# A side-input projection, a variance and a set of stores are moved in a two-layer encoder kernel

## The chip, the core and the metric

The kernel runs on one core of one Trainium2 chip. The metric is the device time of one execution in microseconds (us), and what is reported is the median of several runs. Engines are named as in the profile: PE is TensorE (PEld its weight loads), DVE is VectorE, ACT is ScalarE, POOL is GpSimd, SP is SyncE, which here does nothing but issue DMA transfers. A "q" behind an engine's name (SPq) means its instruction queue: an instruction there issues a transfer and the engine itself stays idle.

## The reference

All is float32; the sequence has 1024 positions, the model 1024 features, and there are two layers. Cut to what matters here, a layer `i` computes

```python
x = layer_norm(ALPHA * x + mix(x), ln_mix_g[i], ln_mix_b[i])        # windowed attention, or HGRN2
x = layer_norm(ALPHA * x + swiglu(x, ffn_w_in[i], ffn_w_out[i]), ln_ffn_g[i], ln_ffn_b[i])
x = x + sigmoid(x @ ple_w_gate[i]) * (p[i] @ ple_w_proj[i])

def layer_norm(x, g, b):
    mu = x.mean(-1); var = square(x - mu).mean(-1)
    return (x - mu) * rsqrt(var + eps) * g + b

def swiglu(x, w_in, w_out):
    g, u = split(x @ w_in, 2)
    return (silu(g) * u) @ w_out
```

The hidden width of the feed-forward part is 2816. The side input `p[i]` has 256 features per position, so `p[i] @ ple_w_proj[i]` needs nothing that the layer computes.

## The kernel before

**Layout.** Activations stand transposed: a tile is 128 features by 512 positions, so a tensor is 8 feature tiles (`m` or `k`, 0 to 7) in two halves `h` of the sequence. For precision every float32 operand of a matmul is split into a rounded part `hi` (an ACT copy to fp32r, line 73) and the rest `lo` (a subtraction on DVE or POOL, line 74); `mm3` (line 317) then makes three matmuls of 512 columns, hi by hi, hi by lo, lo by hi.

**A layer's second part, `ffn_ple` (line 663).** The feed-forward products are made by a seven-product scheme on 2 by 2 blocks (products 1 to 7). The stages are, in order:

- `early` (line 688): products 1 and 2 of the first `NA` = 4 hidden tiles `f`, 24 matmuls each. They need only the first half's normed x and are woven (line 891) with `pend`, the mix norm of the second half.
- `layer_norm` with `which` = 0 and `h` = 1 (line 393; "the mixed norm"): the mean on PE (`mu`), a subtraction on DVE and a square on ACT for each of 8 tiles (lines 400 to 405), the squares added up in `v` by DVE and POOL in turn (line 406), `average(var, ones, v)` (line 411), which splits `v` and makes two matmuls, then square root, reciprocal and scaling. Behind each pair of scaled tiles `combine` (line 367) builds the sums and differences `xc` that products 4 to 7 need, splits them, and stores the four y tiles in DRAM from SP's queue (line 390).
- `matmuls_in` (line 768): for each of 22 tiles `f`, products 6, 5, 7 (`mid`), 4, 3 (`tail`) and from `f` = 4 on 1 and 2 (`head`), 84 matmuls per `f`. Behind each pair of tiles `spill` (line 748) forms four differences on POOL, and `w_sums` (line 757) forms sums of output weights; both lie in a list that `store` (line 763) writes to DRAM from SP's queue. The spill of the last pair and its stores come at the very end (lines 782 to 785).
- `matmuls_out` (line 787): 16 loads bring y back (line 794); then for the seven products `p` in `ORDER` and 11 pairs `k`, 12 matmuls each. `take_w` gives out a weight tile `wo` and a hidden tile `hs`, both loaded from DRAM and split; `wo` lies in the pool `hl` of 5 buffers, `hs` in the pool `x` of 16.
- `ple` (line 853), for each half: it loads and splits the side input (`praw`, `p`), and for each of 8 tiles `m` makes 6 matmuls of the side projection `pr` and 24 of the gate `pgps`, then sigmoid, product and sum. `ple(0)` is woven with the second half's output norm (line 897).

**What sets the order.** Weights come by a plan (`ffn_plan`, `plan_all`): a list of steps with a `begin` that starts a load and a function that splits. `take_w` (line 125) hands out the next step and works ahead by `ahead` steps; a step that has a `begin` may start loading up to three steps before it is split (`fetch_w`, line 115). The `pp` and `pg` weights (lines 286 and 287) have no `begin`. `weave(main, side, ratio)` (line 337) lets one generator take `ratio` steps for each step of the other; the tile framework then orders each engine's instructions by its own estimate, the order written here being its priority, and puts in the waits. Each engine and each queue works strictly in that order. In the trace the mean's matmuls of the first layer stand behind 30 matmuls of `early` although they are written behind 12.

## Time and profile before

| | |
|---|---|
| median of 3 runs | 2908.45 us (2905.96 to 2911.57) |
| profiled execution, its own time | 2906.97 us |
| its span in the trace | 2905.2 us |
| mean granted TensorE clock | 0.972 of full speed |
| instructions | 37125 |
| busy share: PE, DVE, POOL, ACT | 93%, 70%, 48%, 44% |
| HBM read, written | 267.18 MB, 76.02 MB |

A profile is one execution. "Busy" is the time in which an engine's instructions ran; matmuls overlap their neighbours, so each of them is recorded longer than the distance to the next. Where an engine stood idle the trace names what released it (`<-`). The clock column of a stretch (PEclk) is the granted share of full TensorE speed.

### The profile page before, as it was taken

The page shows a single profiled execution, that of the slowest core. Times are in us where ns is not written, and L with a number is a line of the kernel's source. Part 1 is how long each engine was busy: PE and PEld are TensorE (multiplying, and loading weights), DVE is VectorE, ACT ScalarE, POOL GpSimd, SP SyncE. Part 2 cuts the span into 40 slices and gives each one's busy share as a digit, 9 for nine tenths or more (in the row PEclk, how much of TensorE's full clock was granted, in tenths as well). Part 3 has the DMA queues.
Part 4 walks back from the last instruction along what each step waited for, and adds up shares of the span by engine and source line. Part 5 has one row for each costly group of instructions (what it writes and reads, how often), then busy time and mean ns, then how long its engine had stood idle before and what let it go on. Part 6 is the DMA issues. An engine that isn't in the chain of part 4 may idle for free.

```text
span 2905.2 us, 37125 instructions
## 1 busy us (share of the span) xinstructions
PE 2707.3 (93%) x12792; PEld 2175.3 (75%) x12792; DVE 2031.5 (70%) x2949; ACT 1278.9 (44%) x2324; POOL 1384.0 (48%) x968
## 2 busy tenths in 40 slices
PE   8999996999998999999998989989879999989999
PEld 6666774788886877787887878878658888868777
DVE  6778878655554757758888888997885555556674
ACT  4555765233333445544344444444533333434452
POOL 4243245666655446653343433421566655553652
PEclk9999997999999999999999999999979999999999
DMA  4111232544447822221121211112344444496133
GB/s 160 48 44 44 71 129 71 182 152 163 145 160 263 302 73 95 98 85 63 57 64 51 66 55 59 66 48 81 107 141 167 152 152 163 170 342 202 41 108 118
DMA packets 191997, 345.66 MB, mean 119 GB/s; under 512 B 21824, under 2 KB 26688, under 8 KB 191808
## 3 DMA queue, kind: packets, MB, share of 16 engines
q1 hardware_dynamic: 191808, 343.29, 34.7%
q8 instruction: 100, 1.64, 0.2%
q14 instruction: 89, 0.73, 0.1%
HBM read 267.18 MB, written 76.02 MB: 118 GB/s over the span
## 4 chain that ended last, share of the span: by engine, by line
PE 67%; DVE 17%; ACT 5%; issue 4%; POOL 4%; DMA 2%; SPq 0%; ACTq 0%; POOLq 0%; DVEq 0%
PE x L318 5%; PE x L320 5%; PE x L319 5%; PE zy L318 3%; PE zy L320 3%; PE zy L319 2%; PE ox L319 2%; PE ox L320 2%; PE ox L318 2%; PE zps L320 2%; PE zps L319 2%; PE zps L318 2%; PE lv L1019 2%; PE s L525 2%; PE oz L320 1%
## 5 line engine op out<-in xcount | busy, mean ns | idle before, releaser
L74 POOL TENSOR_TENSOR w_hz<-r_hz,w_hz 128x512 fp32r<-128x512 f32 x128 | 180.8, 1420 | 329.3 <-ACT w_hz L73 322.7
L74 POOL TENSOR_TENSOR wo<-wraw,wo 128x512 fp32r<-128x512 f32 x132 | 183.7, 1401 | 230.5 <-ACT wo L73 183.5
L74 DVE TENSOR_TENSOR wp<-wraw,wp 128x512 fp32r<-128x512 f32 x204 | 201.2, 986 | 108.9 <-ACT wp L73 107.9
L74 DVE TENSOR_TENSOR hs<-wraw,hs 128x512 fp32r<-128x512 f32 x154 | 185.0, 1226 | 123.8 <-ACT hs L73 123.6
L318 PE MATMUL x<-xc,wp 128*128 128x512 f32 x528 | 213.4, 405 | 46.4 <-ACT xc L73 41.6
L73 ACT CAST wp<-wraw 128x512 fp32r<-128x512 f32 x204 | 127.0, 622 | 245.0 <-PE zy L320 153.9
L319 PE MATMUL x<-xc,wp 128*128 128x512 f32 x528 | 211.9, 401 | 1.5 <-DVE xc L74 1.5
L318 PE MATMUL zps<-xh_n,w_hz 128*128 128x512 f32 x512 | 212.2, 414 | 0.0
L320 PE MATMUL x<-xc,wp 128*128 128x512 f32 x528 | 211.1, 400 | 0.0
L320 PE MATMUL zps<-xh_n,w_hz 128*128 128x512 f32 x512 | 202.3, 395 | 0.0
L319 PE MATMUL zps<-xl_n,w_hz 128*128 128x512 f32 x512 | 201.0, 393 | 0.0
L73 ACT CAST wo<-wraw 128x512 fp32r<-128x512 f32 x154 | 95.1, 620 | 222.2 <-POOL wo L74 78.7
L318 PE MATMUL ox<-hs,wo 128*128 128x512 f32 x352 | 141.4, 402 | 23.4 <-ACT hs L73 23.4
L318 PEld LDWEIGHTS x<-xc,wp 128*128 128x128 f32 x528 | 100.4, 190 | 79.4 <-ACT xc L73 46.7
L319 PE MATMUL ox<-hs,wo 128*128 128x512 f32 x352 | 141.2, 401 | 1.0 <-DVE hs L74 1.0
L320 PE MATMUL ox<-hs,wo 128*128 128x512 f32 x352 | 140.6, 399 | 0.0
L74 DVE TENSOR_TENSOR wp<-s,wp 128x512 fp32r<-128x512 f32 x88 | 91.8, 1045 | 65.1 <-ACT wp L73 65.0
L1019 PEld LDWEIGHTS lv<-Q,ks 128*128 128x128 f32 x768 | 97.8, 191 | 37.0 <-issue 24.3
L1011 ACT COPY ks<-K 128x512 f32<-128x512 f32 x96 | 60.5, 630 | 145.5 <-DVE K L1016 111.1
L1019 PE MATMUL lv<-Q,ks 128*128 128x128 f32 x768 | 105.4, 279 | 20.3 <-DVE tot L1030 10.3
L319 PEld LDWEIGHTS x<-xc,wp 128*128 128x128 f32 x528 | 100.3, 190 | 27.9 <-DVE xc L74 5.2
L320 PEld LDWEIGHTS x<-xc,wp 128*128 128x128 f32 x528 | 100.4, 190 | 24.4
(373 smaller groups left out, 8444.1 us busy)
## 6 DMA issues: line engine op xcount, KB each, us to landing
wraw<-in_wfi_dram SPq DMA_DIRECT2D x192, 256.0 KB, 5.2
wraw<-in_wfo_dram SPq DMA_DIRECT2D x154, 256.0 KB, 4.7
wraw<-h SPq DMA_DIRECT2D x154, 256.0 KB, 5.3
r_hz<-in_whg_dram SPq DMA_DIRECT2D x128, 256.0 KB, 2.6
wraw<-w SPq DMA_DIRECT2D x88, 256.0 KB, 5.3
w<-wraw SPq DMA_DIRECT2D x66, 256.0 KB, 2.0
h<-th SPq DMA_DIRECT2D x66, 256.0 KB, 2.8
r_pg<-in_wpg_dram SPq DMA_DIRECT2D x64, 256.0 KB, 2.8
```

Of the source, the lines that this page charges most:

```text
L73: act.copy(hi, src)
L74: (eng or dve).tensor_tensor(lo, src, f32(hi), op=ALU.subtract)
L318: pe.matmul(ps, lhsT=w[0], rhs=x[0], start=start, stop=False, skip_group_check=free)
L319: pe.matmul(ps, lhsT=w[0], rhs=x[1], start=False, stop=False, skip_group_check=free)
L320: pe.matmul(ps, lhsT=w[1], rhs=x[0], start=False, stop=stop, skip_group_check=free)
L525: pe.matmul(sp[r][:, :n * P], lhsT=qq[rs], rhs=kk[rs], start=i == 0, stop=i == 2)
L1011: act.copy(view(ks, 0, [[2 * B, g], [B, 2], [1, B]]), kv)
L1019: pe.matmul(lv[:, c], lhsT=ks[:, c * P:(c + 1) * P], rhs=view(Qq, c * P, dims), start=True, stop=True)
```

## The change

- The `pp` weights become plan steps with a `begin`, behind product 2 of `f` = 1. A new generator `shares` loads and splits the side input of both halves, makes the 96 projection matmuls of the layer (each weight tile taken once for both halves), copies each result out of PSUM on ACT and stores it to a DRAM tile `pr`. It runs between `early(1)` and `early(2)`; the weave's ratio goes from 2 to 1.
- `ple` loads `pr` back from DRAM and makes only the 24 gate matmuls per `m`. The `pg` weights get a `begin`: one load per `m` into the pool `x`.
- In the mixed norm each square goes into a plain float32 matmul by the matrix `onef` of 1/1024, summed in PSUM; the additions into `v` and the `average` of it are gone there.
- Stores of y, of the hidden tiles and of the weight sums are issued from ACT's queue instead of SP's, those of the last pair in two parts: two tiles at once, the other five behind the first steps of `matmuls_out`.
- In `matmuls_out` the look-ahead goes from 3 to 6 steps, `wo` moves to the pool `x`, and its split is always POOL's.

```diff
@@ ffn_plan @@
                 one(("w", f, 2), w_src(f, 1))
+                if f == 1:
+                    for m in range(KT):
+                        box = []
+                        def begin(m=m, box=box):
+                            raw = wp.tile([P, 4 * P], F32, tag="raw", bufs=3, name="r_pp")
+                            sync.dma_start(raw[:, :2 * P], wpp[li][m])
+                            box.append(raw)
+                        def fin(box=box):
+                            hl = wp.tile([P, 2, HALF], F32R, tag="hl", bufs=5, name="w_pp")
+                            split(hl[:, 0, :2 * P], hl[:, 1, :2 * P], box[0][:, :2 * P])
...
+                        step(("pp", m), begin, fin)
...
-                        w = blocks(pair_of(box[0], "wo", pool if p not in (7,) else None))
-                        hl = fx["pool"].tile([P, 2, HALF], F32R, tag="x", bufs=16, name="hs")
-                        split(hl[:, 0], hl[:, 1], box[1])
-                        return w, (hl[:, 0], hl[:, 1])
+                        for raw, eng, name in ((box[0], pool, "wo"), (box[1], dve, "hs")):
+                            hl = fx["pool"].tile([P, 2, HALF], F32R, tag="x", bufs=16, name=name)
+                            split(hl[:, 0], hl[:, 1], raw, eng)
...
@@ plan_all @@
-                        will(("pp", m), load_tile, wpp[li], m, 2, "pp")
-                        will(("pg", m), load_tile, wpg[li], m, KT, "pg")
...
+                            raw = fx["pool"].tile([P, 2, HALF], F32, tag="x", bufs=16, name="r_pg")
+                            sync.dma_start(raw.rearrange("p c n -> p (c n)"), wpg[li][m])
...
+                        will2(("pg", m), begin, fin)
@@ combine @@
-                    sync.dma_start(fx["y"][m, h], Y[m][h])
+                    act.dma_start(fx["y"][m, h], Y[m][h])
@@ layer_norm @@
+            mixed = which == 0 and h == 1
+            v = None if mixed else T("to", "v")
+            var = (bank or MM)("var") if mixed else None
...
+                if mixed:
+                    sq = T("t0", "sq")
+                    act.activation(sq, ys[m], AF.Square)
+                    pe.matmul(var, lhsT=onef, rhs=sq, start=m == 0, stop=m == KT - 1)
...
-            var = (bank or MM)("var")
-            average(var, ones, v)
+            if not mixed:
+                var = (bank or MM)("var")
+                average(var, ones, v)
@@ spill, store @@
+                    ts = list(zip(ORDER, (a, c, t2, t3, t4, b, d)))
+                    lag.append([(fx["kept"][p, k], t) for p, t in (ts[2:] if rest else ts)])
...
-                            sync.dma_start(dst, src)
+                            act.dma_start(dst, src)
@@ matmuls_in, at its end @@
+                    store()
+                    act.dma_start(fx["kept"][1, FP - 1], sts[FT - 2]["h"][0])
                     yield from tail(FT - 1, sts[FT - 1])
-                    store()
-                    spill(FP - 1, sts[FT - 2], sts[FT - 1])
-                    store()
+                    act.dma_start(fx["kept"][2, FP - 1], sts[FT - 1]["h"][0])
+                    late.append(lambda: spill(FP - 1, sts[FT - 2], sts[FT - 1], True))
@@ matmuls_out @@
-                            w, hh = take_w("o", p, k, ahead=AHEAD - 1)
+                            if p == 1 and k == 1:
+                                late.pop()()
+                            if p == 1 and k == 4:
+                                store()
+                            w, hh = take_w("o", p, k, ahead=6)
@@ shares (new), ple @@
+                def shares():
+                    pv = {}
+                    for h in range(2):
+                        for k in range(2):
+                            raw = A("praw")
+                            sync.dma_start(raw, pT[li, k * P:(k + 1) * P, h * HALF:(h + 1) * HALF])
+                            hl = hp.tile([P, 2, HALF], F32R, tag="x", bufs=16, name=f"p{k}{h}")
+                            split(hl[:, 0], hl[:, 1], raw)
+                            pv[k, h] = hl[:, 0], hl[:, 1]
+                    yield
+                    for m in range(KT):
+                        w = take_w("pp", m, ahead=3)
+                        for h in range(2):
+                            ps = bank("pr")
+                            for k in range(2):
+                                mm3(ps, w[k], pv[k, h], k == 0, k == 1)
+                            yield
+                            t = A("prs")
+                            act.copy(t, ps)
+                            act.dma_start(fx["pr"][m, h], t)
...
                     for m in range(KT):
-                        wpr = take_w("pp", m)
...
-                            mm3(pr, wpr[k], pv[k], k == 0, k == 1)
-                        yield
-                        ps = yield from lin(take_w("pg", m), xs, "pgps")
+                        pr = T("t1", "pr")
+                        sync.dma_start(pr, fx["pr"][m, h])
+                        ps = yield from lin(take_w("pg", m, ahead=2), xs, "pgps")
@@ ffn_ple @@
                     for f in range(NA):
+                        if f == 2:
+                            yield from shares()
                         yield from early(f)
 
-                weave(all_early(), pend, 2)
+                weave(all_early(), pend, 1)
```

## Rows read from the trace of the kernel before

**Rows 1.** The page's head: the span, and PE's and PEld's lines.

```profile
span 2905.2 us, 37125 instructions
PE 2707.3 (93%) x12792; PEld 2175.3 (75%) x12792; DVE 2031.5 (70%) x2949; ACT 1278.9 (44%) x2324; POOL 1384.0 (48%) x968
```

**Rows 2.** Stretches: from:to, length, busy time (instructions) by engine, clock, DMA.

```profile
429.26:550.24 120.98, 90.47 (x329) 65.94 (x328) 95.95 (x109) 51.72 (x85) 76.53 (x52) 0.83 0.39 134
550.24:883.21 332.97, 332.97 (x1440) 269.90 (x1439) 174.29 (x206) 121.39 (x206) 201.05 (x139) 1.00 0.45 155
883.21:949.00 65.79, 53.52 (x218) 42.26 (x217) 29.59 (x29) 23.30 (x40) 32.66 (x23) 0.90 0.81 290
949.00:1142.54 193.54, 189.02 (x798) 149.88 (x796) 124.84 (x128) 90.59 (x156) 101.39 (x73) 0.99 0.46 160
1142.54:1261.13 118.59, 113.94 (x485) 92.61 (x484) 85.66 (x92) 64.00 (x111) 70.54 (x49) 0.97 0.29 93
2070.13:2189.11 118.98, 86.88 (x330) 64.28 (x328) 95.92 (x109) 49.24 (x81) 75.78 (x52) 0.86 0.36 126
2189.11:2900.10 710.99, 689.14 (x2937) 553.89 (x2935) 405.56 (x452) 288.11 (x494) 379.94 (x262) 0.98 0.47 161
```

**Rows 3.** PE's waits, 429 to 560: total us, times, longest.

```profile
PE x L318 <- ACT xc L73: 19.5, 4, 7.1
PE var L364 <- ACT avh L73: 6.0, 1, 6.0
```

**Rows 4.** The mixed norm's chain on DVE and ACT, from the timeline.

```profile
442.52 3.07 DVE L400 TENSOR_TENSOR y<-y,mu 128x512 f32<-128x512 f32 x5
...
456.78 0.62 ACT L73 CAST avh<-v 128x512 fp32r<-128x512 f32 x1 [1.74 <-POOL v L406]
...
460.42 0.69 ACT L413 ACTIVATE rs<-var,eps 128x512 f32<-128x512 f32 x1 [1.72 <-PE var L365]
```

**Rows 5.** The stretch of the mixed norm alone, columns as in Rows 2.

```profile
438.50:498.00 59.50, 32.76 (x95) 21.89 (x94) 52.18 (x60) 34.77 (x56) 29.09 (x20) 0.68 0.21 71
```

**Rows 6.** Side projection and side input: duration min/median/max, first and last start.

```profile
L318 PE MATMUL pr<-p,w_pp x64: 393/397/400, 1142.5 to 2893.9; 128*128 128x512 f32 x64
...
L73 ACT CAST w_pp<-r_pp x32: 387/406/408, 1131.6 to 2883.8; 128x256 fp32r<-128x256 f32 x32
L74 DVE TENSOR_TENSOR w_pp<-r_pp,w_pp x32: 411/690/1511, 1132.0 to 2884.3; 128x256 fp32r<-128x256 f32 x32
...
L74 DVE TENSOR_TENSOR p<-praw,p x8: 678/1174/1750, 1135.0 to 2835.3; 128x512 fp32r<-128x512 f32 x8
```

**Rows 7.** A PSUM copy on ACT: the groups, count, busy us, mean ns, idle before.

```profile
L717 ACT COPY u<-x 128x512 f32<-128x512 f32 x72 | 42.3, 587 | 125.5 <-PE x L320 125.5
```

**Rows 8.** Plain float32 matmuls of 128 columns and their neighbours: start, us, from the timeline.

```profile
1301.10 1.05 PE L1019 MATMUL lv<-Q,ks 128*128 128x128 f32 x8
1301.91 0.36 PE L956 MATMUL hvps<-w_hv,xh_n 128*128 128x256 f32 x1
```

**Rows 9.** SP's queue where the output products begin: start, us, from the timeline.

```profile
905.10 0.38 SPq L766 DMA_DIRECT2D h<-g  x1
908.19 0.32 SPq L766 DMA_DIRECT2D h<-h  x1
...
915.13 9.53 SPq L794 DMA_DIRECT2D y<-y  x16
924.99 0.33 SPq L146 DMA_DIRECT2D wraw<-in_wfo_dram  x1
```

**Rows 10.** PE's waits from 883 to 1262, as in Rows 3.

```profile
PE ox L318 <- ACT hs L73: 11.8, 1, 11.8
PE pgps L320 <- DVE w_pg L74: 4.1, 1, 4.1
PE oz L319 <- DVE hs L74: 3.0, 1, 3.0
```

**Rows 11.** SP's longest wait from 1000 to 1200.

```profile
SPq L857 <- PE var L365: 55.4, 1, 55.4
```

**Rows 12.** Waits from 550 to 883: SP's stores, and ACT's copies (560 to 880).

```profile
SPq L766 <- DVE g L740: 113.9, 16, 7.7
...
ACT u L717 <- PE x L320: 60.4, 34, 2.1
```

More of the change, by code (lines that the diff above doesn't have):

```diff
@@ L208, in ffn_plan @@
                 one(("w", f, 2), w_src(f, 1))
+                if f == 1:
[8 more added lines that the diff above has]
+                            split(hl[:, 0, :2 * P], hl[:, 1, :2 * P], box[0][:, :2 * P])
+                            return [tuple(hl[:, i, k * P:(k + 1) * P] for i in range(2)) for k in range(2)]
+                        step(("pp", m), begin, fin)
             tails = {}
@@ L285, in ffn, with begin, fin @@
                     for m in range(KT):
-                        will(("pp", m), load_tile, wpp[li], m, 2, "pp")
-                        will(("pg", m), load_tile, wpg[li], m, KT, "pg")
+                        box = []
+                        def begin(m=m, box=box):
+                            raw = fx["pool"].tile([P, 2, HALF], F32, tag="x", bufs=16, name="r_pg")
+                            sync.dma_start(raw.rearrange("p c n -> p (c n)"), wpg[li][m])
+                            box.append(raw)
+                        def fin(box=box):
+                            r = []
+                            for c in range(2):
+                                hl = fx["pool"].tile([P, 2, HALF], F32R, tag="x", bufs=16, name="w_pg")
+                                split(hl[:, 0], hl[:, 1], box[0][:, c])
+                                r += blocks((hl[:, 0], hl[:, 1]))
+                            return r
+                        will2(("pg", m), begin, fin)
             def z(i, n):
@@ L416, in layer_norm @@
                 yield
-            mixed = which == 0 and h == 1
             for m in [m + i for m in range(KH) for i in (0, KH)] if mixed else range(KT):
@@ L670, in ffn_ple @@
                 fx["kept"] = {(p, k): D_(f"h{p}_{k}") for p in ORDER for k in range(FP)}
+                fx["pr"] = {(m, h): D_(f"pr{m}{h}") for m in range(KT) for h in range(2)}
                 fx["sums"] = {(p, k): D_(f"w{p}_{k}") for p in (3, 5, 6, 7) for k in range(FP)}
@@ L746, in tail, with spill @@
                     st["h"] = h0, h1
-                def spill(k, sa, sb):
+                def spill(k, sa, sb, rest=False):
                     (a, b), (c, d) = sa["h"], sb["h"]
@@ L754, in spill @@
                     pool.tensor_tensor(t4, c, t2, op=ALU.subtract)
-                    lag.append([(fx["kept"][p, k], t) for p, t in zip(ORDER, (a, c, t2, t3, t4, b, d))])
+                    ts = list(zip(ORDER, (a, c, t2, t3, t4, b, d)))
+                    lag.append([(fx["kept"][p, k], t) for p, t in (ts[2:] if rest else ts)])
                 def w_sums(k):
@@ L781, in matmuls_in @@
                             w_sums(f // 2)
+                    store()
+                    act.dma_start(fx["kept"][1, FP - 1], sts[FT - 2]["h"][0])
                     yield from tail(FT - 1, sts[FT - 1])
[L783 to L785 removed]
+                    act.dma_start(fx["kept"][2, FP - 1], sts[FT - 1]["h"][0])
+                    late.append(lambda: spill(FP - 1, sts[FT - 2], sts[FT - 1], True))
+                late = []
                 def matmuls_out():
```

15 lines of the change are left out of this document (4 added, 11 removed).

## The prediction

> **What bounds the kernel now.** I read the page's head first, then the work by stretch, then the waits of the weak stretches, and last the timeline of the queues in them. The head says that PE is busy for 93% of the span [rows 1], so the 198 us in which it is not, and what it runs at a low clock, are all that can be won without removing work. Where they lie the stretches tell. From 550 to 883 PE never stops and holds its full clock [rows 2]; by the code it makes 17 times 84 = 1428 matmuls there, so one costs 332.97 / 1428 = 0.2332 us, and I use that as the ideal price everywhere. The five stretches of the first layer then compare like this (matmuls by the code):
>
> - A, `early` and the mixed norm, 429 to 550: 328 matmuls, 76.5 us, took 120.98: 44.5 us lost, at a granted clock of 0.83 (of 2.4 GHz, a mixture of both levels).
> - B, start of the output products: 228 matmuls, 53.2 us, took 65.79: 12.6 lost.
> - C, the other output products: 796 matmuls, 185.6 us, took 193.54: 7.9 lost.
> - D, `ple`: 484 matmuls, 112.9 us, took 118.59: 5.7 lost.
>
> The second layer repeats it: A took 118.98, so 42.5 lost; the rest, 2936 matmuls or 684.7 us, took 710.99, 26.3 lost [rows 2]. Together 139.5 us, the ceiling of any gain here. In A the waits show why: PE stands four times for the split `xc`, 19.5 us, and once for the variance, 6.0 [rows 3]. The norm's chain on DVE, ACT and POOL ends last, while PE has run out of `early`. In B it waits 11.8 us for a hidden tile [rows 10].
>
> **The change part by part, for one layer.**
>
> *Projection moved.* 8 tiles, 2 halves, 2 chunks, 3 products are 96 matmuls of the ordinary kind [rows 6], 96 x 0.2332 = 22.4 us. They leave D, where PE is the bound, and go to A, where it idles. The idle time must hold them: from 429.3 PE would have 96 + 96 matmuls, 44.8 us, the mean, 0.5, and the new variance matmuls. A plain float32 matmul of 128 columns shows as two rows; four of them take from 1301.10 to 1301.91 or a little more, at most 0.23 each, so one of 512 columns about 0.92, eight 7.4 us [rows 8]. That ends at 482, and the norm's stretch ended at 498 [rows 5]. It fits, if the norm is no slower.
>
> *The norm's own time.* From the first subtraction at 442.5 to the square root at 460.4 it takes 17.9 us now, with additions alternating between two engines and a split of the sum [rows 4]. Eight squares feeding eight matmuls of 0.92 would take some 9: 8.5 us shorter. Against that stands what is added to ACT in the same stretch: 16 PSUM copies of 0.59 = 9.4 [rows 7], 16 stores of `pr` and 16 of y at SP's 0.32 to 0.38 an issue = 11.2 [rows 9], 8 casts of 0.41 and 4 of about 0.6 = 5.7 [rows 6], less one split of 0.6. ACT's 34.8 us in 59.5 become 60.5; DVE's 52.2, plus 8 x 0.69 and 4 x 1.17, less three additions and a split of the same shape, some 3.8, become 58.6 [rows 5, 6]. Both are full. The four side-input tiles also take places in the pool `x`, so the last four `xc` wait for the end of the projection; by PE's order it ends well before them. So I let the stretch end 5 us later instead of 8.5 earlier; it is nearest to the engine sums, with some waits in order. Low end of the cost: minus 8.5; high end: none of the new ACT work finds a hole, 25.7 less 8.5 = 17.2. Gain of A and D together: 22.4 - 5 = 17.4.
>
> *Stores off SP, deeper look-ahead, B.* SP stands at the last pair's stores from 905.1 to 915.1, held by POOL's and DVE's results; only then come 16 loads of y, 9.5 us, and the next weight load at 924.99 [rows 9]. Without those stores all of it can move up by 10.0 us, and with more pairs loaded ahead nearly the whole wait of 11.8 goes: 11. What comes next is the y loads, which need free buffers. The last spill's four POOL operations are now beside product 1, whose pairs do not read them.
>
> The Trainium skill, "DMA: Bandwidth & Descriptors", section "Issuing engines are not separate DMA queues", says that transfers from all engines share the same DMA engines and that a second issuing engine only saves issue time. By that rule B would gain seven issues of 0.32, 2.3 us, and the sum below would be 17 us smaller. The trace does not bear this out as the limit here, since SP's 10 us are waits for producers and not transfers; I keep the row.
>
> *C and D.* In C PE waits 3.0 for a hidden tile [rows 10], behind a stand of 55.4 us of SP at the side input's load, which wants a buffer [rows 11]; that load is gone from there. Six pairs ahead and one in use are 14 of the 16 buffers of `x`. Product 7's 11 splits of `wo` come to POOL, busy for 101 of 194 [rows 2], which covers them. 5.5 of 7.9 gained, between 0 and 7.9. In D a late gate weight costs 4.1 [rows 10]; its load now starts steps ahead. But the second half's norm must finish beside 8 x 24 matmuls, 44.8 us, instead of 56.0, helped by 8 x 0.69 + 2 x 1.17 = 7.9 less on DVE [rows 6]. Gain 3; between 5.7 and 7.9 - 11.2 = -3.3. Reading `pr` back adds 16 loads on SP, each issued a whole gate product ahead, 5.6 us; without that cover each would cost its wait.
>
> *The long middle stretch.* 11 pairs with 7 and 4 stores each, some 110 issues of 0.33, put 36 us on ACT, which is busy for 121 of 333 [rows 2]. Its holes hide them. Behind a store wait the PSUM copies (L717), for which PE has 12 matmuls, 2.8 us less 0.59, so 2.2 us of slack; ACT arrives early at these copies by 60.4 / 34 = 1.8 us on average [rows 12]. I take 2.5 us lost; bounds 0 and the last rival.
>
> *Sum.* 17.4 + 11 + 5.5 + 3 - 2.5 = 34.4 a layer, 68.8 for two. The profiled execution took 2906.97 us, 1.8 more than its span; 2838.2, and the median of the runs stands 1.5 above it: 2840.
>
> **The rivals.**
>
> *Everything fits.* The norm takes its full 8.5 less and all other losses go: 22.4 + 8.5 + 12.6 + 7.9 + 5.7 = 57.1 a layer, 2794. For it: PE's 16 us of room. Against: DVE at 88% in that stretch already [rows 5].
>
> *ACT and DVE become the bound of A.* The stretch ends 17.2 later and D's norm sticks out by 3.3: 22.4 - 17.2 + 11 + 5.5 - 3.3 - 2.5 = 15.9 a layer, 2877. For it: the two sums above their stretch. Against: ACT's holes in it are waits of the kind that the change removes.
>
> *Slower: ACT stands at the stores.* The place is the store of a hidden tile behind DVE's product (L740). SP waits there 16 times, 7.1 us each [rows 12]; if ACT comes to it as early, splits and copies stand behind it, and PE loses 7.1 - 2.2 = 4.9. Ten pairs in two layers, 98 us: 2840 - 5 + 98 = 2933. It decides against the change from 73.8 / 20 = 3.7 us a pair, that is when ACT comes 5.9 us early. Against: SP is early because it has nothing else to do; ACT has work that is written ahead of the store.
>
> The Trainium skill, "DMA: Bandwidth & Descriptors", section "Anatomy of one DMA", says the same as a rule: any semaphore wait is served by the issuing sequencer before the transfer is dispatched. Rows of SP agree; of ACT's queue the trace of before has none.
>
> *The stores were not what held SP.* If the y loads wait for buffers until the last tiles are through, the queue move does nothing and B gains 2.3 as by issue alone: 2857.
>
> **How the numbers follow.** Forecast 0.55 (its own range 2815 to 2862), everything fits 0.12, A bound by ACT and DVE 0.15, slower 0.09, stores not the cause 0.08, something within 0.2% 0.01. A difference under 0.2%, 6 us, is about what a measurement of this kernel can't tell from none. From 2792 to 2880 the range takes in all but the slower case and the edges: some 0.8. Faster: 0.55 + 0.12 + 0.15 + 0.08 = 0.90; same 0.01; slower 0.09.
>
> **What would show it.** In the profile after: PE busy between 440 and 480 without the 6.0 us wait, `xc` waits shorter than 19.5 in sum, and the last `xc` near 503; the wait of 11.8 for `hs` gone and the y loads before 910; no SP wait at a side-input load; the middle stretch still at 0.233 a matmul. I am wrong if that stretch gets longer than 333 us by over 10, if A's stretch grows by more than the 22.4 that it took in, or if PE waits for the second half's output norm in `ple`.

## The result, and the profile after

The changed kernel takes 2869.35 us (median of 4 runs, 2863.95 to 2873.5) against 2907.2 for the kernel before on the same chip: a ratio of 0.9867, 95% interval 0.9844 to 0.9889. It is faster by 38 us, and the forecast was 67. The profiled execution took 2872.11 us, 34.9 less than that of before.

The page's head, which answers to [rows 1]: 35 us less span, with PE busy for 4 us more than before.

```profile
span 2870.3 us, 37158 instructions
PE 2711.7 (94%) x12820; PEld 2184.5 (76%) x12820; DVE 2007.5 (70%) x2903; ACT 1287.1 (45%) x2338; POOL 1407.1 (49%) x982
```

The stretches after, with the columns of [rows 2]. In order: A, the middle, B, C and D of the first layer, then A, B, C and D of the second.

```profile
429.50:559.80 130.30, 114.51 (x439) 85.25 (x438) 97.36 (x116) 63.70 (x111) 75.56 (x51) 0.95 0.55 184
559.80:892.77 332.97, 332.97 (x1440) 270.25 (x1439) 171.45 (x206) 121.33 (x206) 192.70 (x136) 1.00 0.45 155
892.77:955.98 63.21, 53.24 (x219) 42.45 (x217) 28.67 (x26) 23.77 (x43) 39.97 (x27) 0.92 0.78 262
955.98:1146.89 190.91, 183.54 (x798) 150.20 (x796) 130.98 (x124) 96.19 (x165) 123.17 (x86) 0.99 0.57 197
1146.89:1245.37 98.48, 95.31 (x388) 75.34 (x389) 68.77 (x63) 48.29 (x80) 65.61 (x45) 0.96 0.24 75
2056.22:2189.49 133.27, 115.65 (x439) 86.38 (x438) 100.98 (x117) 62.81 (x109) 75.45 (x50) 0.94 0.51 173
2522.46:2579.18 56.72, 52.53 (x218) 41.58 (x217) 28.07 (x27) 22.97 (x40) 32.97 (x22) 0.97 0.80 277
2579.18:2769.29 190.11, 184.01 (x798) 150.08 (x796) 128.99 (x123) 94.54 (x163) 123.61 (x86) 0.99 0.56 192
2769.29:2865.10 95.81, 93.16 (x388) 73.71 (x388) 60.82 (x66) 40.68 (x66) 41.53 (x29) 0.98 0.37 122
```

For the second layer [rows 2] had one row for all that follows A. Split in the same way, the trace of before has B, C and D there as:

```profile
2522.08:2587.60 65.52, 53.37 (x218) 42.12 (x217) 29.74 (x29) 23.28 (x40) 32.67 (x23) 0.90 0.80 287
2587.60:2781.59 193.99, 189.28 (x798) 149.84 (x796) 121.50 (x128) 90.35 (x156) 101.35 (x73) 0.99 0.46 158
2781.59:2900.10 118.51, 113.52 (x485) 92.01 (x483) 76.55 (x90) 53.09 (x92) 44.02 (x29) 0.97 0.34 115
```

Held against the forecast, in us gained per layer:

| stretch | forecast | first layer | second layer |
|---|---|---|---|
| A, takes in the projection | -5 | -9.3 | -14.3 |
| D, gives it up | 22.4 + 3 | 20.1 | 22.7 |
| B | 11 | 2.6 | 8.8 |
| C | 5.5 | 2.6 | 3.9 |
| middle | -2.5 | 0.0 | 0.0 |
| sum | 34.4 | 16.0 | 21.1 |

The two layers gain 37.1; the stretch of hgrn (the second layer's mixer) between them is 1.9 longer in this execution, and some tenths lie at the ends. One wait stands in the wrong row of this table: D is counted from the first gate product, and PE stands 4.3 us in the first layer and 1.8 us in the second ahead of that product (rows below), so that this wait falls into C. With it put where it belongs, C gained 7.0 and 5.7 us, and D 15.8 and 20.9.

What PE waits for has changed in kind. First A (429 to 560), then B to D of the first layer (892 to 1246), columns as in [rows 3]:

```profile
PE za L349 <- ACT prs L917: 4.2, 1, 4.2
PE x L349 <- DVE u L757: 4.0, 3, 2.5
PE x L351 <- DVE wp L74: 2.0, 1, 2.0
PE pr L349 <- ACT prs L917: 1.9, 1, 1.9
```

```profile
PE ox L349 <- ACT hs L73: 9.3, 1, 9.3
PE pgps L349 <- DVE y L864: 4.3, 1, 4.3
PE pgps L350 <- POOL xl L74: 2.3, 3, 1.1
```

and B to D of the second layer (2522 to 2866):

```profile
PE ox L349 <- ACT hs L73: 2.9, 1, 2.9
PE pgps L349 <- DVE y L864: 1.8, 1, 1.8
PE pgps L350 <- POOL xl L74: 1.8, 3, 0.9
```

The 19.5 us for `xc` and the 6.0 for the variance [rows 3] are gone from A. In their place PE stands at banks (of PSUM, which take matmul results) that the projection's copies (`prs`) have not emptied, and at DVE. In B the wait for a hidden tile is 9.3 in the first layer, where it was 11.8 [rows 10], and 2.9 in the second. At the start of D there is a new one: the first gate product wants a bank that the last output product holds until DVE's line 864 has read it.

### The profile page after: what moved, and what is told of

Its sections match the earlier page's. It is cut to its first block, busy times and chain, and to the rows that moved or that the text cites. A ratio compares the mean times of both kernels' runs of the same rounds, so it can differ in the third digit from the quotient of the medians.

```text
span 2870.3 us, 37158 instructions
## 1 busy us (share of the span) xinstructions
PE 2711.7 (94%) x12820; PEld 2184.5 (76%) x12820; DVE 2007.5 (70%) x2903; ACT 1287.1 (45%) x2338; POOL 1407.1 (49%) x982
## 4 chain that ended last, share of the span: by engine, by line
PE 33%; DVE 11%; issue 5%; POOL 4%; DMA 3%; ACT 2%; SPq 0%; ACTq 0%; POOLq 0%; DVEq 0%
PE x L349 3%; PE x L351 3%; PE x L350 3%; PE zps L351 2%; PE zps L350 2%; PE zps L349 2%; PE lv L1078 2%; POOL wo L74 2%; PE op L1158 1%; DVE K L1075 1%; PE zy L349 1%; PE zy L351 1%; PE zy L350 1%; DMA wraw<-w 1%; DVE Q L1048 1%
## 5 line engine op out<-in xcount | busy, mean ns | idle before, releaser
L74 DVE TENSOR_TENSOR wp<-wraw,wp 128x512 fp32r<-128x512 f32 x204 | 216.0, 1059 | 167.0 <-ACT wp L73 137.9
L74 DVE TENSOR_TENSOR hs<-wraw,hs 128x512 fp32r<-128x512 f32 x154 | 206.3, 1356 | 144.7 <-ACT hs L73 141.5
L74 POOL TENSOR_TENSOR wo<-wraw,wo 128x512 fp32r<-128x512 f32 x154 | 226.2, 1481 | 157.4 <-ACT wo L73 153.5
L186 POOL TENSOR_TENSOR wraw<-s,wraw 128x512 f32<-128x512 f32 x36 | 47.6, 1322 | 217.4 <-DVE wp L74 204.8
L349 PE MATMUL ox<-hs,wo 128*128 128x512 f32 x352 | 138.7, 397 | 12.2 <-ACT hs L73 12.2
L351 PE MATMUL ox<-hs,wo 128*128 128x512 f32 x352 | 139.0, 395 | 1.6 <-POOL wo L74 1.6
L350 PE MATMUL ox<-hs,wo 128*128 128x512 f32 x352 | 139.1, 395 | 0.4 <-DVE hs L74 0.4
L349 PEld LDWEIGHTS x<-xc,wp 128*128 128x128 f32 x528 | 100.4, 190 | 34.7 <-ACT wp L73 5.8
L351 PEld LDWEIGHTS x<-xc,wp 128*128 128x128 f32 x528 | 100.4, 190 | 29.4 <-DVE wp L74 4.8
L73 ACT CAST w_hz<-r_hz 128x512 fp32r<-128x512 f32 x128 | 79.0, 618 | 89.6 <-issue 42.4
```

The source lines that it names most:

```text
L73: act.copy(hi, src)
L74: (eng or dve).tensor_tensor(lo, src, f32(hi), op=ALU.subtract)
L186: pool.tensor_tensor(a11, tmp, a11, op=ALU.subtract)
L349: pe.matmul(ps, lhsT=w[0], rhs=x[0], start=start, stop=False, skip_group_check=free)
L350: pe.matmul(ps, lhsT=w[0], rhs=x[1], start=False, stop=False, skip_group_check=free)
L351: pe.matmul(ps, lhsT=w[1], rhs=x[0], start=False, stop=stop, skip_group_check=free)
```

## The experiments

Every kernel here is the changed kernel with the edit shown; none leaves out any of the computation. They were run on several chips, each beside the kernel before, so the whole is compared by the ratios; e_early and e_early_sp have two runs each, the others four or five. The stretches are those of one execution each. A run-to-run difference of the whole of some 5 us (the changed kernel's own runs lie 2864 to 2874) is as large as some of the effects, so each is read in its stretches first. The middle is 332.97 us in both layers of every one of these kernels, to the hundredth. Stretches in which the granted clock falls are less steady: D of the first layer came out between 94.8 and 98.3 us in kernels whose edit does not touch it. A difference under 4 us in one stretch is therefore taken as an effect only where a wait goes or comes with it. Here C and D are one column, from the end of B to the end of the last gate product.

| kernel | median us | ratio to before, interval | A, two layers | B | C and D |
|---|---|---|---|---|---|
| before | 2907.2 | | 121.0, 119.0 | 65.8, 65.5 | 312.1, 312.5 |
| changed | 2869.35 | 0.9867 (0.9844 to 0.9889) | 130.3, 133.3 | 63.2, 56.7 | 289.4, 285.9 |
| e_sp | 2876.2 | 0.9891 (0.9876 to 0.9906) | 133.6, 136.5 | 61.6, 57.7 | 286.7, 285.7 |
| e_early | 2884.89 | 0.9919 (0.9900 to 0.9937) | 129.8, 133.8 | 70.0, 63.5 | 287.4, 285.6 |
| e_early_sp | 2894.38 | 0.9951 (0.9933 to 0.9969) | 134.4, 136.8 | 71.4, 64.6 | 287.5, 285.8 |
| e_ahead | 2879.94 | 0.9900 (0.9885 to 0.9915) | 130.2, 133.7 | 59.7, 58.5 | 293.8, 289.5 |
| e_tie | 2863.68 | 0.9848 (0.9833 to 0.9863) | 129.4, 133.5 | 56.8, 56.9 | 291.3, 284.3 |
| e_bank | 2866.35 | 0.9857 (0.9840 to 0.9873) | 130.3, 133.3 | 62.4, 56.6 | 287.1, 283.8 |
| e_var | 2885.54 | 0.9918 (0.9901 to 0.9934) | 139.1, 138.4 | 62.2, 57.2 | 289.1, 286.8 |
| e_ple | 2867.36 | 0.9853 (0.9837 to 0.9869) | 115.7, 116.4 | 59.1, 57.6 | 301.1, 299.3 |
| e_half | 2862.89 | 0.9842 (0.9829 to 0.9856) | 124.3, 128.2 | 58.4, 58.4 | 290.9, 289.9 |
| e_prs | 2866.44 | 0.9862 (0.9846 to 0.9879) | 129.4, 128.4 | 62.6, 56.3 | 285.1, 287.7 |
| e_pool | 2874.26 | 0.9881 (0.9866 to 0.9896) | 132.3, 134.9 | 62.7, 56.9 | 285.1, 287.5 |
| e_best | 2860.11 | 0.9836 (0.9822 to 0.9850) | 128.3, 131.2 | 56.8, 57.0 | 284.6, 283.7 |

### e_sp: the stores back on SP's queue

```diff
-act.dma_start(...)     # the five store statements, lines 421, 805, 822, 824, 918
+sync.dma_start(...)
```

> All stores that the change put on ACT's queue go back to SP, nothing else. Two questions. (1) The stretch A (first matmul of early to the start of the long middle, 130.3 and 133.3 us in the changed kernel). Theory ACT: A grew because ACT's in-order queue carries 32 more issues of 0.33 us among the PSUM copies; then A gets shorter by 5 to 10 us a layer here. Theory buffers: A is held by tiles of the pool of 48 that come free only when their stores have landed; then A stays within 4 us of what it was, or gets longer where loads stand behind stores. (2) The start of the output products, B (63.2 and 56.7 us). As forecast, moving the stores off SP was worth up to 10 us there: then B is 70 or more in the second layer. If the stores were not what held SP, B stays within 3 us. The middle stretch, 332.97 us, stays as it is by either, since SP has nothing else to do there. Total by buffers and by the forecast for B: 15 to 25 us slower than the changed kernel; by ACT: 0 to 15 faster.

A is 3.3 and 3.2 us longer, so ACT's extra issues are not what lengthened it: theory ACT falls. B of the second layer is 57.7 against 56.7, and B of the first is even shorter. Alone, the queue is worth 1.0 us there, not the ten that I had put on it. By the medians some 7 us of the whole (0.0024 of 2908) stand behind the queue, but the two intervals overlap. The place is A, which is longer with the stores on SP under the late and under the early spill (e_early_sp against e_early: 4.6 and 3.0 us). What SP stands at in A of e_sp (429.7 to 563) are the projection's results and a hidden tile, with weight loads behind them; the y stores cost it little:

```profile
SPq L918 <- ACT prs L917: 29.3, 11, 10.1
SPq L805 <- DVE g L774: 25.5, 3, 13.6
```

### e_early and e_early_sp: the last spill ahead of the output products

```diff
-late.append(lambda: spill(FP - 1, sts[FT - 2], sts[FT - 1], True))
+spill(FP - 1, sts[FT - 2], sts[FT - 1], True); store()
...
-if p == 1 and k == 1:
-    late.pop()()
-if p == 1 and k == 4:
-    store()
```

e_early_sp has the five statements of e_sp on SP as well.

> The last pair's spill and its stores are put back ahead of the output products, but on ACT's queue; all else as in the changed kernel. So far, in the second layer (no next layer's loads in the queue), B is 56.7 us, 57.7 with all stores on SP and 58.5 with the short look-ahead, against 65.5 before. Theory either way: it is enough that these stores don't stand ahead of the y loads in one queue, whether by another queue or by a later place; then B of the second layer is 56 to 58 here. Rival POOL: the four operations of the last spill hold up the first weight parts on POOL; then B is 60 or more here. Whole within 5 us of the changed kernel by the first, 5 to 10 slower by the second.

> As the kernel before this one in the list (spill and stores ahead of the output products), with all stores on SP's queue: both halves of the step are undone, look-ahead and the rest stay. Theory either way: now SP stands at the stores ahead of the y loads again, and B of the second layer is 62 to 66, as it was before the change; with the rows of the other three, that shows that the forecast's stand of SP was the cause and that the change removes it twice. Rival: the rest of the change (weight parts in the large pool, six pairs ahead) gave the gain, and B stays at 59 or less.

The second layer's B makes a square: late on ACT 56.7, late on SP 57.7, early on ACT 63.5, early on SP 64.6. The place in the program is worth 6.8 or 6.9 us, the queue 1.0 or 1.1. The theory that one of the two suffices is refuted by the third number.

The Trainium skill, "DMA: Bandwidth & Descriptors", section "Issuing engines are not separate DMA queues", says that a second issuing engine saves issue time alone. By that rule the forecast had 2.3 us here, and these runs agree with the rule and not with the row that I preferred to it.

Why the queue does not help is in SP's waits of e_early, second layer, 2529 to 2593, with PE's below them:

```profile
SPq L836 <- DMA h<-g: 8.1, 1, 8.1
SPq L836 <- DMA h<-h: 6.2, 2, 4.3
```

```profile
PE ox L349 <- ACT hs L73: 10.9, 1, 10.9
```

SP no longer stands at the stores, but the y loads (line 836) need places in the pool of 48 (the SBUF tiles that `A` gives out), and these are held by the hidden tiles until their stores have landed. The stand has moved from the store to the load behind it. What the later spill changes shows in SP's queue, too: the 16 y loads and the first weight load behind them, in the changed kernel and then in e_early (second layer; the middle stretch ends at 2522.5 and at 2529.2):

```profile
2540.01 13.98 SPq L836 DMA_DIRECT2D y<-y  x16
2554.95 0.33 SPq L146 DMA_DIRECT2D wraw<-in_wfo_dram  x1
```

```profile
2543.20 24.73 SPq L836 DMA_DIRECT2D y<-y  x16
2568.02 0.91 SPq L146 DMA_DIRECT2D wraw<-in_wfo_dram  x1
```

The weight load comes 32.5 and 38.8 us after the end of the middle stretch, 6.3 us of the 6.8. In the four kernels of the square it comes at 32.5, 33.5, 38.8 and 41.0 (late on ACT, late on SP, early on ACT, early on SP), and B ends 23.6 to 24.7 us after it in each: B is as long as the y loads hold SP up. The expectation's rival, POOL held up by the last spill, is not it, although B is over its 60: in e_early POOL waits for ACT's half of the weight parts, and ACT for loads.

```profile
POOL wo L74 <- ACT wo L73: 29.2, 4, 15.5
```

### e_ahead: look-ahead of three pairs, weight parts in the small pool

```diff
-w, hh = take_w("o", p, k, ahead=6)
+w, hh = take_w("o", p, k, ahead=AHEAD - 1)
```

(and `fin` of the output products as before the change)

> The look-ahead of the output products goes back from six pairs to three, and the weight parts to the small pool where they were before; all else as in the changed kernel. The queue move has turned out to give the start of the output products (B) nothing. Theory: the deeper look-ahead is what gave B its 8.8 us in the second layer (65.5 to 56.7); B goes back to between 62 and 66 there, C (190.1) to about 194, and the whole is 10 to 17 us slower than the changed kernel. Rival: the last spill's delay behind the first pairs gave it; then B stays within 2 us of 56.7, and the whole within 5.

C and D are 4.4 and 3.6 us longer, although most of the wait ahead of the first gate product is gone here; without that wait C alone is 7.6 and 5.4 longer, about what it had gained. The hidden tile's wait of before [rows 10] is back, to the tenth, in both layers:

```profile
PE oz L348 <- DVE hs L74: 3.0, 1, 3.0
```

No side input is loaded in C of this kernel, so SP's stand at that load [rows 11] was not what this wait hung on. The edit undoes three things at once (look-ahead, pool, the split of product 7), which were not told apart. B of the second layer is 58.5 and not 62 to 66: its gain is the late spill's, and the rival was right within its 2 us. For the whole, its bound of 5 us was too small: 0.0033 of 2908 are 9.6. The first layer's B is 3.5 us shorter here: in this kernel the fourth weight load of hgrn is issued at 1146.1 us and not at 904.9, so that none stands ahead of the y loads (see e_tie).

### e_tie: the next stage's loads kept out of the queue

```diff
 # load_w, only for the first three weight loads of hgrn
+dve.tensor_copy(raw[:, :1], fx["tie"][:, :1])     # fx["tie"] = Y[2][1], ready in the second half of ple
 sync.dma_start(raw[:, :n], src)
```

> The first three weight loads of hgrn get one element from a tile that is ready only late in ple, so that these loads can't stand early in SP's queue (in the changed kernel they stand in it from 461 us on, between the wfi loads and again at the start of the output products). Theory: they are what costs the first layer's B its gain, because SP stands at them; B of the first layer falls from 63.2 to about 57, what the second layer has, where no hgrn follows; A of the first layer is at most 3 us shorter; the second layer is unchanged; the whole is 5 to 9 us faster, less 0 to 2 at hgrn's start. Rival: B waits for buffers that the last hidden tiles and the y tiles hold; then B stays within 1 us of 63.2 and the whole within 2.

B of the first layer falls from 63.2 to 56.8, that of the second stays: theory right, to the number. These loads are an effect of the change that I did not see in the diff. It took `ple`'s weights out of the three `raw` buffers (into which weights are loaded), so that nothing stands between the projection's weights and those of hgrn any longer, and the latter were moved up in SP's queue by hundreds of us (the first is issued at 460.9 us; before the change, at 1246.2). SP in the changed kernel, where the first layer's output products begin (start, us, from the timeline):

```profile
904.89 0.33 SPq L79 DMA_DIRECT2D r_hv<-in_wvh_dram  x1
...
909.74 6.40 SPq L79 DMA_DIRECT2D r_hz<-in_whg_dram  x2
916.19 0.45 SPq L836 DMA_DIRECT2D y<-y  x1
```

For 6.4 us SP is at two weights of hgrn, whose stretch starts 335 us later, and the y loads start behind them, at 916.19. That is 23.4 us after the end of the middle stretch; it was 31.9 before (915.13 [rows 9], less 883.21), and in e_tie it is 17.6, against 17.5 in the second layer of both kernels.

### e_bank: other banks for the first gate products

```diff
-ps = yield from lin(take_w("pg", m, ahead=2), xs, "pgps")
+ps = bank("pgps") if h == 0 and m < 3 else MM("pgps")
+yield from lin_steps(take_w("pg", m, ahead=2), xs, ps)
```

> The first three gate products of ple's first half take banks of the pool of five, which nothing else needs there, instead of the pool of three that the last output product still holds. Theory: the waits of 4.3 and 1.8 us of the first gate product for DVE (which was beside the projection's matmuls before) go, and D gets 4 to 6 us shorter over both layers. Rival: the norm is what ends last there, PE then stands at the next wait (the split of the second half's normed tile, 2.3 and 1.8 now), and D gains under 2 us.

The gate products take their banks from a pool of three (`MM`); the edit gives the first three of them banks of another pool, of five (`bank`). The waits for DVE's line 864 are gone, and C and D together are 2.3 and 2.1 us shorter: 4.4 of the 6.1 that the two waits took. In the first layer, from 1138 to 1244, others now come first:

```profile
PE mu L395 <- ACT avh L73: 2.5, 1, 2.5
PE pgps L350 <- POOL xl L74: 2.0, 2, 1.3
```

The first is the start of the norm that runs beside `ple`, so the bank was most of this loss, and behind it stands the norm.

### e_var: the squares summed on DVE and POOL again

```diff
-if mixed:
-    sq = T("t0", "sq")
-    act.activation(sq, ys[m], AF.Square)
-    pe.matmul(var, lhsT=onef, rhs=sq, start=m == 0, stop=m == KT - 1)
-elif m == 0:
+if m == 0:
...
-if not mixed:
-    var = (bank or MM)("var")
-    average(var, ones, v)
+var = (bank or MM)("var")
+average(var, ones, v)
```

> The mixed norm's squares are added on DVE and POOL again, as before the change, and no matmul of PE sums them; all else as in the changed kernel. If the norm's own chain sets the end of A, A gets longer by 5 to 9 us a layer (the chain from the first subtraction to the square root was 17.9 us and is 10.6 now). If what ends A are buffers, DVE and the loads that come after the square root, or if the eight plain matmuls (6.9 us of PE) cost what the chain gains, A moves by less than 3 us either way. Whole: 10 to 18 slower, or within 6.

A is 8.8 and 5.1 us longer, and the whole some 15 us slower. The square root starts 31.6 us after the start of A (at 431.4) and not 22.0:

```profile
L445 ACT ACTIVATE rs<-var,eps x1: 688/688/688, 463.0 to 463.0; 128x512 f32<-128x512 f32 x1
```

So a later norm does make A longer, and summing on PE is the part of the change that gains most there.

### e_ple: the projection back in ple

```diff
-if f == 2:
-    yield from shares()
...
-pr = T("t1", "pr")
-sync.dma_start(pr, fx["pr"][m, h])
+wpr = take_w("pp", m)
+pr = fps.tile([P, HALF], F32, tag="f", name="pr")
+for k in range(2):
+    mm3(pr, wpr[k], pv[k], k == 0, k == 1)
+yield
```

(with the two weight plans as before the change, and the loads of the side input at the head of `ple`)

> The projection goes back into ple, with no copies and no stores of it in A; all else as in the changed kernel. D gets longer by the 20.1 and 22.7 us that it had gained. A: if the norm's chain alone bounds it, it is what it was before less the shorter chain, 121 and 119 less about 7: 112 to 114, and the move is worth 2 to 7 us a layer, so this kernel is 5 to 14 us slower than the changed one. If the projection's copies, splits and buffers hold up the norm as well, A falls further, to 105 to 110, and the move is worth nothing or costs something.

It is as fast as the changed kernel (0.9853 against 0.9867). Moving the projection, the step of the largest term in the forecast, gives nothing on top of the other parts. (The move alone, on the kernel before, was not run.) Its A and D of the first layer (D from the first gate product on), and PE's wait in A:

```profile
427.16:542.84 115.68, 93.03 (x343) 66.31 (x342) 91.39 (x104) 50.93 (x83) 73.97 (x51) 0.87 0.43 147
...
1124.52:1235.80 111.28, 111.28 (x478) 89.63 (x477) 70.90 (x79) 58.11 (x102) 68.89 (x49) 1.00 0.26 86
```

```profile
PE x L335 <- ACT xc L73: 18.8, 4, 7.7
```

Two things are to be seen. D has no wait at all, in either layer, and a clock of 1.00: the other parts of the change had already taken away what D lost, and the projection was work that covered the second half's norm and the first banks. When it leaves, C and D shrink by 11.7 and 13.4 us and not by 22.4. And A, whose idle time was to swallow 22.4 us, grows by 14.6 and 16.9. A was at 115.7 and not at the 112 to 114 that I expected, so neither of the two theories of the expectation has its numbers; the sum, no gain from the move, is the second's. The stretches overstate it: the profiled executions of the two kernels differ by 11.8 us and their medians by 2.0, so up to 10 us of these differences belong to the single executions, and no gain is what is shown, not a loss. (Of the first layer's difference 4.1 us are B's: with the projection's weights in `ple` again, hgrn's loads can't pass them.)

### e_half: half of the projection in A

```diff
 # shares(): only the second half of the side input
-for h in range(2):
+for h in (1,):
...
 # ple(h): as in e_ple for h == 0, reads pr back for h == 1
```

(the eight results in three buffers of their own)

> Only the projection of the second half of the side input is moved to A (8 products and 8 stores a layer instead of 16, in three buffers of their own); that of the first half stays in ple, beside the second half's norm. With the whole projection in ple, A was 115.7 and 116.4 us and D had no wait at all (111.3 to its last gate product); with all of it in A, A was 130.3 and 133.3 and D 98.3 and 95.6, with waits of 7.5 and 4.5 us. Theory: in the first half of ple the projection is the cover of the second half's norm, and in A PE is full once some 11 us are added; then A is 117 to 123, D about 100 to 102 with no wait, and the whole is 8 to 20 us faster than the changed kernel, 2849 to 2861, and 0 to 10 faster than the three edits together. Rival: A's cost is not a matter of how much is added, but of the norm being disturbed at all; then A is 126 or more, and the whole is at 2865 or above.

D has no wait in the second layer and 0.9 us in the first, as the theory of the cover says. A refutes the other half: with 11.2 us of matmuls added it grows by 8.6 and 11.8, to 124.3 and 128.2, around the rival's 126; the whole, 2862.9, lies between the two theories' numbers. Held against e_ple, A of the two layers is 20.4 us longer and C and D 19.6 shorter, so moving half of it gains nothing either. How the norm goes on after its square root shows why. Start of the square root (ACT), and last start of POOL's four `xc` (of sixteen; DVE's last starts at most 0.4 us later in these kernels), in the first layer of the changed kernel, of e_ple and of e_half, in this order:

```profile
L451 ACT ACTIVATE rs<-var,eps x1: 687/687/687, 451.5 to 451.5; 128x512 f32<-128x512 f32 x1
...
L74 POOL TENSOR_TENSOR xc<-tx,xc x4: 1394/1560/1571, 467.8 to 501.8; 128x512 fp32r<-128x512 f32 x4
```

```profile
L437 ACT ACTIVATE rs<-var,eps x1: 688/688/688, 453.3 to 453.3; 128x512 f32<-128x512 f32 x1
...
L74 POOL TENSOR_TENSOR xc<-tx,xc x4: 1350/1425/1563, 469.6 to 490.9; 128x512 fp32r<-128x512 f32 x4
```

```profile
L453 ACT ACTIVATE rs<-var,eps x1: 689/689/689, 451.6 to 451.6; 128x512 f32<-128x512 f32 x1
...
L74 POOL TENSOR_TENSOR xc<-tx,xc x4: 1547/1562/1574, 468.2 to 501.5; 128x512 fp32r<-128x512 f32 x4
```

From the square root to POOL's last `xc`: 50.3, 37.6 and 49.9 us. Half a projection delays the norm's second part as much as a whole one, by 12 us; before the change it took 36.5. In e_half PE then waits for `xc` again, 12.6 us; in the changed kernel it has the other half to do and comes too late instead.

### e_prs and e_pool: two tries at the delay

```diff
 # e_prs
-t = A("prs")
+t = hp.tile([P, HALF], F32, tag="prs", bufs=1, name="prs") if (2 * m + h) % 3 == 2 else T("t2", "prs")
```

```diff
 # e_pool: low parts of w_pp and p
-split(hl[:, 0], hl[:, 1], raw)
+split(hl[:, 0], hl[:, 1], raw, pool)
```

> The 16 projection results of a layer (prs) wait for their store in three buffers of their own instead of the pool of 48; the count of instructions and of ACT's issues is the same. Theory buffers: wfi loads and the norm's tx tiles get their places earlier, the waits of 4.2 to 4.5 us for prs copies shrink, A is shorter by 5 to 10 us a layer and the whole by 10 to 20. Theory ACT (its queue carries too many copies and issues): A stays within 2 us, and so does the whole. A third way: three buffers are too few, and the copies wait for their own stores (2.0 to 5.7 us from issue to landing); then A gets longer.

> The low parts of the projection's weights and of the side input (8 of 0.7 and 4 of 1.2 us on DVE) are made by POOL, which in the changed kernel has nothing to do from 444 to 460 us. Theory: DVE, busy for nearly all of 452 to 468 and 500 to 524, sets A's end together with SP's stand at the third buffer for projection weights (17 to 23 us behind a DVE split); then A gets shorter by 5 to 10 us a layer. Rival: A is set by buffers and by ACT's queue; within 2 us. Third: POOL's own tiles of the norm (tx) come later, and A gets longer.

With buffers of their own for `prs` the part from the square root to the last `xc` is 47.7 us instead of 50.3 (450.1 to 497.8), and in the second layer 46.1 instead of 48.3, so the pool of 48 is a piece of it, though a small one. A gained 0.9 and 4.8, less than the 5 to 10 of the theory, and PE's idle time in it did not fall: the longest wait only has another name.

```profile
PE za L349 <- ACT w L73: 6.1, 1, 6.1
```

The shorter A of the second layer shows in PE's busy time (112.0 for 115.7), that is in the clock. With the low parts on POOL, DVE is 3.3 us less busy and A 2.0 and 1.6 us longer: theory DVE, in this form, is refuted. POOL waits for ACT with them:

```profile
POOL w_pp L74 <- ACT w_pp L73: 15.7, 5, 4.9
```

What makes the other 10 us of the delay stays open. One reading that no run tested: the projection stands between the second and the third of `early`'s four columns, so the weights of the last two (`w`, four splits on DVE and four on ACT) are made after the square root, between the norm's own operations; in e_ple none of them lies there, in e_half and in the changed kernel all four do.

### e_best: the three edits that helped, together

The edits of e_prs, e_tie and e_bank.

> The three edits that helped, together: three buffers of their own for the projection's results, the first hgrn loads tied to a late tile, the first three gate products in the pool of five banks. If they act in different places, as the stretches say: A 0.9 and 4.8 us shorter, B of the first layer 6.4, the start of D 2.3 and 2.1: 16 to 17 us in sum, so about 2853. If one hides another (the earlier start of D meets the norm's end, a shorter A of the second layer meets a later load), 8 to 12: about 2859.

At 2860.1 us (0.9836, 0.9822 to 0.9850) it is the fastest of these kernels by median. Its interval overlaps that of the changed kernel (0.9844 to 0.9889) at the edge, and those of e_half and e_tie widely, so it is not shown to be faster than these two. The layers are 13.3 and 4.1 us shorter, where the single edits add up to 9.6 and 6.9; hgrn's stretch came out 2.6 longer. The time is that of the second theory of the expectation, 2859.

## Why the prediction came out as it did

The direction was right, and the range held the time, being wide. Of the 67 us forecast, 38 came, and not from where most of them were expected: A and D together, the projection's move, were to give 17.4 + 3 us a layer, and e_ple shows that the move gives nothing on top of the rest. What made the kernel faster were the sum on PE, the place of the last spill and the deeper look-ahead. By the forecast's steps, against the measured execution:

- **The norm's own time: right in the first layer, and it misled me.** I wrote that its chain would be 8.5 us shorter, that the stretch would end 5 us later, and that the last `xc` would be near 503. The square root starts 8.9 us earlier (451.5 for 460.4 [rows 4]), and the last `xc` starts near 502 and ends at 503.7. Counted from the start of A, the last `xc` ends 5.2 us later in the first layer and 8.3 in the second. The term of 5 us was the norm's, but A does not end with the norm. The failed step is "It fits, if the norm is no slower": I took the ordering of PE's work for free. In the changed kernel PE has 422 ordinary matmuls and 8 of 0.86 us in A, 104.5 us at the full clock; the records show it busy for 114.5 and idle for 15.8. The larger part of the excess of 10.0 is low clock: a mean of 0.95 over 130.3 us is some 13 us at the lower level, a loss of at most 6.5. From the end of the last `xc` to the end of A it needs 4.2 and 6.0 us more than before. So A cost 9.3 (5.2 + 4.2, rounded) and 14.3 (8.3 + 6.0), the second near the 17.2 of the rival in which ACT and DVE bound it.
- **The gain of D: too high.** Where 25.4 was forecast, 15.8 and 20.9 were measured; the 20.1 and 22.7 of the table come near the forecast only because a wait ahead of D is counted in C. In e_ple D, the projection in it, is 5.9 and 5.8 us shorter than before, so that much, all of my upper bound of 5.7, came from the other parts of the change; which of them was not told apart, but the wait of 4.1 for a gate weight [rows 10] is gone. The projection's leaving gave 11.7 and 13.4, C counted in, and not 22.4. The step that failed is that the 22.4 us "leave D, where PE is the bound": PE stays the bound only as long as the norm of the second half and the banks of the last output product hide behind PE's work, and the projection was part of that cover.
- **B: wrong in its cause, and in its size for the first layer.** The step "Without those stores all of it can move up by 10.0 us" held the queue to be the cause. The queue gives 1.0, the later place of the last spill 6.8. The rival "the stores were not what held SP", chance 0.08, described the mechanism: the y loads wait for buffers. In the second layer the size, 8.8 of 11, came near the forecast, but by luck: the queue that it was built on gave 1.0 of it. In the first layer another 6.4 us went to the loads of hgrn, which I had not looked for.
- **C: right in its size, in part wrong in its cause.** 5.5 taken, 7.0 and 5.7 measured when the wait ahead of D is left out. The gain comes from the look-ahead with the pool that went with it (e_ahead), not from the side input's load having left SP's queue.
- **The middle stretch: a cost of 2.5 taken, none measured.** The stores on ACT (94 of them in the stretch, not some 110) are hidden completely. With that the slower rival, ACT standing at the stores, falls.
- **The price of a matmul: slightly wrong.** The middle stretch holds 1440 matmuls, as [rows 2] shows, not 1428, so one costs 332.97 / 1440 = 0.2312 us; the missing 12 were counted in B, which has 216. B before thus lost 15.9 us and not 12.6, and C 9.5 and not 7.9. No term of the sum hangs on it but the 22.4, which would be 22.2.

Of the signs of being wrong that the prediction named, one came: PE waits in `ple` for the second half's output norm (`xl`), 2.3 and 1.8 us. Of the signs that it was right, two did not come in the first layer: the wait for `hs` stayed at 9.3 us, and the y loads start at 916.19 and not before 910.

The misses by term, first and second layer, are 4.3 and 9.3 in A, 9.6 and 4.5 in D, 8.4 and 2.2 in B, less 1.5 and 0.2 in C, less 2.5 twice; with hgrn's 1.9 that is 33.6 (before rounding) of the 33.9 by which the gain of the profiled execution, 34.9, fell short of 68.8.

Where the 38 us come from, the undone parts tell by their ratios (the changed kernel's taken off, times 2908): the sum on PE 15, the later spill 15, the look-ahead 10, the queue 7, the moved projection -4. They sum to 42 (before rounding) and not to 38; parts that share a stretch need not add up. Each is uncertain by some 8 us, most of that being the changed kernel's own interval, which is common to all of them; for the projection and for the queue that includes zero. The weave's ratio and the earlier gate weights were undone in no run.

## What to carry to other kernels

Work that is taken from a stretch bound by PE may be the cover of something: before moving it, list what waits behind it there (norms, banks, late loads), and count the gain only down to the next of these. A queue that stands at a store is often standing for buffers; if so, another queue moves the stand to the next load, and only a later place or a free buffer takes it away. When a change frees a small ring of load buffers, look for what will be pulled up into it.

## What the runs showed that was not expected

- Stores issued by ACT cost PE nothing where ACT has holes: with 94 issues of 0.33 to 0.48 us added to ACT's queue, the middle stretch is 332.97 us, as before. (ACT's busy time, 121.33 against 121.39 [rows 2], does not count issues.) One of them:

```profile
605.13 0.33 ACTq L805 DMA_DIRECT2D h<-g  x1
```

- A plain float32 matmul of 512 columns shows as two rows and takes 0.86 us: from 445.68 to 447.63 PE does two of them and one ordinary matmul, (1.95 - 0.23) / 2. The forecast had 0.92.

```profile
445.68 1.88 PE L437 MATMUL var<-sq,onef 128*128 128x512 f32 x4
447.00 0.80 PE L351 MATMUL za<-xh,w 128*128 128x512 f32 x1
447.63 0.59 PE L437 MATMUL var<-sq,onef 128*128 128x512 f32 x1
```

- The granted clock fell behind waits that are quite short. In the changed kernel's A:

```profile
468.00:476.00 8.00, 6.11 (x27) 4.58 (x26) 6.40 (x8) 6.30 (x12) 4.84 (x3) 1.00 0.80 270
476.00:484.00 8.00, 7.48 (x21) 5.41 (x20) 4.08 (x5) 5.15 (x9) 2.34 (x3) 0.57 0.93 309
```

PE idles for 1.9 of the first eight us, is busy for 7.5 of the next eight, and gets 0.57 of 2.4 GHz there, which is mostly the lower level, 1.2. Such stretches are most of the 10.0 us by which PE's busy time in A exceeds its 104.5, and they make it vary: in e_best PE is idle for 16.3 and 15.7 us of the two A's, and busy for 112.0 and 115.5.
